# The seam between two stages of a one-core decoder layer: rotary rows, first loads, last stores and four merge tiles change their places

## The chip, the core and the metric

The kernel runs on one core of a Trainium2 chip. A core has a matrix engine (TensorE, PE in the profile), a vector engine (VectorE, DVE), a scalar engine (ScalarE, ACT), a general one (GpSimd, POOL) and a sync engine (SyncE, SP) that here does nothing but issue transfers. Each engine works through its own list of instructions in order; semaphores hold it up where it needs another's result. ACT and POOL can issue transfers too. The metric is the device time of one execution in microseconds; the number that counts is the median of several runs.

## What is computed

One layer of a decoder. x has 1024 rows of 1024 channels; 16 learned rows are put ahead of them, so L = 1040.

```python
h = rms_norm(h_res, pre_norm_g)
z = h @ w_in                       # 1024 x 7328, cut into branches and gates
y_a = (pool_mixer(pv, ...) * silu(pg)) @ w_out_pool
y_b = (mla_attention(cq, ckv, kr, ...) * silu(mg)) @ w_out_mla
y_c = (conformer_conv(cu, ...) * silu(cg)) @ w_out_conf
y_d = (short_conv(sbcx, ...) * silu(sg)) @ w_out_sc
m = sum_i sigmoid(gl_i + bias_i) * y_i
out = h_res + rms_norm(m @ w_o, post_norm_g)     # the 16 rows are dropped
```

The attention has 8 heads of 64 + 32 channels, the 32 being rotary: a rotated key part that all heads share. It is causal, and its softmax is exact (the row maximum is taken off).

## The kernel before, in words

All matmuls are done in a split form: an operand is written as a rounded part and a rest, and three matmuls make one product. The work has three stages, each recorded first and then put in order by a planner.

*Stage one* makes z: 28 pairs of column blocks, each by a scheme of seven block products instead of eight (`unit`, line 578). The last 16 pairs are the merge gates: 32 tiles `th` of 128 channels by 1024 rows, a tanh by ACT each, stored to DRAM by `out_gate` (line 682). Its line 689 issues those stores from ACT, but for the last pair (g == 30) from POOL. Beside the products run the convolutions, the pooling, the queries, keys and values, and the splitting of later weights. Branch results (`bo`), `q`, `k`, the shared rotary key rows `kr`, and `v` with its ones all go through DRAM.

*Stage two* (from line 1244) is the attention, 8 heads by two halves of 512 queries: `seq` (line 1451). For each, `maxima` (line 1302) takes row maxima of the scores: PE, then DVE with a mask made by POOL, then a transpose on PE and a copy by ACT into four further rows of the query tile `qt`. Then `attend` (line 1339): scores, exp, the split of the probabilities, the product with the values. `load_q` fetches a query tile (three buffers), `load_kv` (line 1290) a head's keys `kt` (two buffers), rotary rows and values `vt` (two buffers). The rotary rows are loaded once for each key buffer: for h == 0 into the first, for h == 1 into the second, there with the two halves of the rows exchanged. Between the steps of the attention runs the merge of the three other branches, the generator `fills` (line 1417): 48 steps, each six matmuls (`ps_y`) and an evacuation by DVE with the gate tile `th`. A gate tile and a weight tile `whl` serve two steps; `load_bo` fetches the branch's two operands of 1024 KB each. `refill` (line 1455) hands out the steps evenly over the attention and, with `plan.ahead(-400)`, behind the attention in priority.

*Stage three* merges the attention's branch and makes the output product.

**The planner** (`Plan`, line 194). `record` notes each operation with its engine, a cost, its dependencies and a priority, the number of the record less what `ahead` adds. `behind` (line 248) makes everything recorded inside it wait for the last PE operation recorded so far; lines 1483 to 1490 use it so that the loads for the next head and the next but one query tile don't run ahead of the attention's current step. `flush` (line 334) goes through time, gives each engine the ready operation of the lowest number that `fits`, and emits all operations in that order; stage one is emitted whole before stage two. `fits` (line 367) keeps back a transfer of SP or ACT while the eighth last such transfer has not landed by the planner's reckoning (`landed`, line 417); transfers of POOL are left out of that list. The reason lies in the program: each transfer that SP or ACT issues takes one of eight completion semaphores in turn, and waits until the one that had it before has landed; POOL's take others.

Memory is laid out by pools, and stage two's tiles lie where stage one's lay. A load into such a place waits until the last work there is over.

Of the kernel before, what the change touches and what calls it, by code (L numbers as in the profile page):

```python
# [14 lines left out]

# [49 lines left out]
def f(ap):  # L65
    return ap.bitcast(F32)
# [127 lines left out]
class Plan:  # L194
# [139 lines left out]
    def flush(self):  # L334
# [26 lines left out]
        def slot(b, t):  # L361

            free = [sl for sl in b.group["slots"] if not sl["live"] and sl["after"] <= t]
            if free and (b.group["any"] or b.group["order"][b.group["next"]] is b):
                return min(free, key=lambda sl: (sl["after"], sl["i"]))

        def fits(o, t):

            if o["op"] == "dma_start" and o["eng"] != "POOL" and len(self.landed) >= 8 and self.landed[-8] > t:
                return False  # L370
            return all(slot(b, t) for b in o["bufs"] if not b.live and b.group)

        while events:
            t = events[0][0]
            while events and events[0][0] <= t:
                _, kind, i = heapq.heappop(events)
                if kind == 0:
                    o = self.ops[i]
                    bisect.insort(ready[o["eng"]], (o["prio"], o["i"]))
                elif kind == 2:  # L380
                    for b in self.ops[i]["bufs"]:
                        b.left -= 1
                        if b.left == 0 and b.group:
                            b.slot["live"], b.slot["after"] = None, t
            for e in self.free:
                if self.free[e] > t:
                    continue
                o = next((self.ops[i] for _, i in ready[e] if fits(self.ops[i], t)), None)
                if o is None:
                    if e == "PE" and self.idle and self.ops[self.idle[1]]["end"] is None:  # L390
                        order.append(self.idle[0])
                        self.free[e] = t + 160
                        heapq.heappush(events, (self.free[e], 1, 0))
                    continue
                ready[e].remove((o["prio"], o["i"]))
                for b in o["bufs"]:
                    if not b.live:
                        b.live = True
                        if b.group:
                            b.slot = slot(b, t)  # L400
                            b.slot["live"] = b
                            b.group["next"] += 1
                o["start"] = t
                if o["turns"]:
                    o["cost"] += max(0, self.port[{"DVE": "POOL", "POOL": "DVE"}[e]] - t) * 0.7
                    self.port[e] = t + o["cost"]
                self.free[e] = t + o["cost"]
                o["end"] = t + o["cost"] + self.WAKE[e]
                if o["op"] == "dma_start":
                    if self.pipe is None:  # L410
                        self.pipe = max((x["done"] for x in self.ops if x["op"] == "dma_start"
                                         and "done" in x and x["start"] <= t), default=0)
                    o["done"] = self.pipe = max(self.pipe, t) + o["bytes"]
                    land = self.pipe + o["bytes"] + 4500 + min(0, o["extra"])
                    o["end"] = land + max(0, o["extra"])
                    if o["eng"] != "POOL":
                        self.landed.append(land)
                    heapq.heappush(events, (land, 1, 0))
                for b in o["bufs"]:
                    b.last = max(b.last, o["end"])  # L420
                order.append(o)
                heapq.heappush(events, (self.free[e], 1, 0))
                heapq.heappush(events, (o["end"], 2, o["i"]))
                for u in o["users"]:
                    u["need"] -= 1
                    same = u["eng"] == e and o["op"] != "dma_start"
                    u["at"] = max(u["at"], self.free[e] if same else o["end"])
                    if not u["need"]:
                        heapq.heappush(events, (u["at"], 0, u["i"]))
# [8 lines left out]
def trunk_kernel(ctx, tc, a):  # L438
    nc = tc.nc
    plan = Plan(nc)  # L440
    PE, ACT, DVE, POOL, SP = (plan.engine(e) for e in ("PE", "ACT", "DVE", "POOL", "SP"))
# [7 lines left out]
    def ld(out, in_):  # L449
        SP.dma_start(f(out) if out.dtype == F32R else out, f(in_) if in_.dtype == F32R else in_)  # L450
# [38 lines left out]
    th_dram = [dram.tile([P, NT], F32, name=f"th{i}") for i in range(32)]  # L489
# [6 lines left out]
    kr_dram = dram.tile([32, 2, L], F32R, name="kr")  # L496
# [136 lines left out]
    def full(to, x, ps):  # L633

        if x is None:
            copy(to, ps)
        else:
            add(DVE, to, ps, x)

    def pairs_of_halves(n, each, store):  # L640

        z = {}

        def out(i, j, ps, x, tmp):
            first = i not in z
            if first:
                z[i] = up.tile([P, 2, n], F32, tag="z", bufs=2, name="z")
            m = ps.shape[0]
            each(i, z[i][:m, j], ps, x, tmp)
            if not first:  # L650
                store(i, z[i][:m])
        return out
# [11 lines left out]
    def row(t):  # L664
        return t.rearrange("p j n -> p (j n)")
# [16 lines left out]
    def out_gate(g):  # L682

        def each(i, to, ps, x, tmp):
            if x is not None:
                full(to, x, ps)
            ACT.activation(to, ps if x is None else to, AF.Tanh, scale=0.5,
                           bias=par[:, R_GB + g + i:R_GB + g + i + 1])
        return pairs_of_halves(512, each, lambda i, t: (POOL if g == 30 else ACT).dma_start(th_dram[g + i], row(t)))

# [587 lines left out]
    def load_q(h, c):  # L1280
        qt[h, c] = qk.tile([NA, 2, 512], F32R, tag="q", bufs=3, name="qt")
        ld(qt[h, c][:QK].rearrange("p s n -> p (s n)"), q_dram[c][h].rearrange("p s n -> p (s n)"))

    load_q(0, 0)
    kt = [qk.tile([NA, 2, L], F32R, name=f"kt{i}") for i in range(2)]
# [4 lines left out]
    def load_kv(h):  # L1290
        e, k_, v_ = h % 2, kt[h % 2], vt[h % 2]
        ld(k_[:64].rearrange("p s n -> p (s n)"), k_dram[h // 2][64 * e:64 * (e + 1)].rearrange("p s n -> p (s n)"))
        if h == 0:
            ld(k_[64:96], kr_dram)
        if h == 1:
            ld(k_[64:80], kr_dram[16:])
            ld(k_[80:96], kr_dram[:16])
        v = v_dram[h // 4][h % 4]
        ld(v_[:, 0:8].rearrange("p j c -> p (j c)"), v[:, 0:8].rearrange("p j c -> p (j c)"))
        ld(v_[:NM, 8], v[:NM, 8])  # L1300
# [95 lines left out]
    op, smg = {}, {}  # L1396
# [53 lines left out]
    fill = fills()  # L1450
    seq = [(h, c) for h in range(H) for c in range(2)]
    NUNIT = 16 * 7
    count = {"u": 0, "f": 0}

    def refill():
        count["u"] += 1
        while count["f"] < min(48, 48 * count["u"] / (NUNIT - 2)):

            with plan.ahead(-400):
                next(fill, None)  # L1460
            count["f"] += 1
# [9 lines left out]
    def lead_to(i, n=0):  # L1471

        while lead["i"] <= min(i, len(seq) - 1) or lead["steps"] < n:
            if next(steps, "end") == "end":
                lead["steps"] = math.inf
            lead["steps"] += 1

    load_kv(0)
    load_q(*seq[1])
    lead_to(0)  # L1480
    units = 0
    for i, (h, c) in enumerate(seq):
        with plan.behind():
            if i + 2 < len(seq):
                load_q(*seq[i + 2])
            if c == 0 and h + 1 < H:
                load_kv(h + 1)
            if c == 0 and h % 2:
                smg[h] = at.tile([P, NT], F32, tag="smg", name="smg")
                ld(smg[h], z_dram[f"mg{h // 2}"])  # L1490
        for _ in attend(h, c):
            units += 1
            lead_to(-1, min(5 + units * 10 / 14, 5 * (i + 3)))
            refill()
        lead_to(i + 1)
        with plan.ahead(-300):
            if h == H - 1:
                head_out(h, c, sums_pe(h, c))
            elif c:
                for k, rb in enumerate(sums(h)):  # L1500
                    head_out(h, k, rb)
# [82 lines left out]
    for d in (0, 4, 1, 5, 2, 6, 3, 7):  # L1584
# [3 lines left out]
        for c in range(2):  # L1588
            t = th[:, 512 * c:512 * (c + 1)]
# [23 lines left out]
    def half(name, bufs=4):  # L1613
        return ep.tile([P, 512], F32, tag=name, bufs=bufs, name=name)
# [71 lines left out]
    for t in range(4):  # L1686

        parts = [slice(0, 512)] if t < 3 else [slice(0, 256), slice(256, 512)]
        g = half("g", 1) if t == 3 else a_[t]
# [45 lines left out]
```

## Time and profile before

| | us |
|---|---|
| median of 3 runs | 1018.12 |
| lowest, highest | 1017.72, 1019.06 |
| the profiled execution | 1017.58 |
| its span, first to last instruction | 1015.9 |
| PE busy | 990.5 |
| PE's last matmul of stage one ends | 651.6 |
| PE works on stage three alone from | 883.4 |

The execution is 1.7 us longer than its span. The line numbers of the profile are of no use here: the planner issues every operation from line 332, so the groups are told apart by tiles. A row of the timeline holds the start, the length, the engine, the operation with output and inputs, the count, and in brackets how long the engine stood before it and what it waited for. `SPq`, `ACTq` mark the issue of a transfer, and the length there is that of the issue alone. A row of waits holds who waited for whom, the total in us, how often, and the longest.

### The profile page before, as it was taken

To read this page: it belongs to the slowest core of one execution; us is meant where nothing else is said; L and a number is where in the kernel's file an instruction comes from. 1 tells how busy PE (TensorE), PEld (TensorE's weight loads), DVE (VectorE), ACT (ScalarE), POOL (GpSimd) and SP (SyncE) were. 2 spreads that over 40 slices of the span, in tenths; PEclk is the share of its full clock that TensorE was granted. 3 is DMA by queue.
4 is the path that set the end of the run, shared out by engine and by line. 5 is a ranking of instruction groups with operands and counts; after the bars stand their busy time and mean duration, and the time that the engine had idled before them with its cause. 6 is when DMAs were issued, how large, how long until landed. Compare 5 with 4: busy or idle time off the path is not lost.

```text
span 1015.9 us, 15303 instructions
## 1 busy us (share of the span) xinstructions
PE 990.5 (98%) x5139; PEld 831.7 (82%) x5139; DVE 668.1 (66%) x1106; ACT 455.4 (45%) x911; POOL 685.6 (67%) x640
## 2 busy tenths in 40 slices
PE   9999999999999999999999999989999999799996
PEld 9999898889888878887877888868887878588885
DVE  6754795997999499435455453255565675598747
ACT  7632234443354544444534444136556556224632
POOL 6767867766777666768776765125678876556956
PEclk9999999999999999999999999989999999899998
DMA  7278755679767856566656456877568671662634
GB/s 246 75 229 277 245 169 182 217 226 301 250 214 224 288 189 206 188 197 203 206 175 197 136 172 191 310 206 241 147 188 256 183 209 53 201 228 89 202 120 165
DMA packets 126302, 203.13 MB, mean 200 GB/s; under 512 B 19650, under 2 KB 79161, under 8 KB 124880
## 3 DMA queue, kind: packets, MB, share of 16 engines
q1 hardware_dynamic: 121600, 185.38, 58.2%
q10 hardware_dynamic: 4336, 15.73, 4.2%
q8 instruction: 40, 0.66, 0.3%
q0 software_dynamic: 288, 1.05, 0.3%
q14 instruction: 38, 0.31, 0.1%
HBM read 128.40 MB, written 73.72 MB: 199 GB/s over the span
## 4 chain that ended last, share of the span: by engine, by line
PE 91%; DVE 4%; issue 2%; DMA 1%; POOL 1%; ACT 1%; SPq 0%; DVEq 0%; POOLq 0%; ACTq 0%
PE ps_pa L332 16%; PE ps_pb L332 16%; PE ps_pc L332 15%; PE ps_o L332 10%; PE ps_y L332 8%; PE ps_s L332 7%; PE ps_pd L332 7%; PE ps_u L332 7%; PE ps_x L332 4%; DMA kt<-kr 1%; DVE x L332 1%; DVE a L332 1%; DMA x<-in_x_dram 0%; DVE ps_w L332 0%; DVE ss L332 0%
## 5 line engine op out<-in xcount | busy, mean ns | idle before, releaser
L332 PE MATMUL ps_pb<-T,S 128*128 128x512 f32 (+2 forms) x792 | 172.4, 362 | 0.8 <-DVE u L332 0.8
L332 PE MATMUL ps_pa<-B,A 128*128 128x512 f32 (+2 forms) x792 | 172.2, 362 | 0.0
L332 POOL TENSOR_TENSOR S<-ss,S 128x512 fp32r<-128x512 f32 x84 | 110.5, 1328 | 76.9 <-ACT S L332 76.7
L332 PEld LDWEIGHTS ps_pa<-B,A 128*128 128x128 f32 x792 | 134.6, 188 | 24.4 <-issue 0.5
L332 PEld LDWEIGHTS ps_pb<-T,S 128*128 128x128 f32 x792 | 133.8, 188 | 24.4 <-DVE u L332 1.2
L332 POOL TENSOR_TENSOR A<-raw,A 128x512 fp32r<-128x512 f32 x84 | 116.9, 1397 | 48.2 <-ACT A L332 44.7
L332 POOL TENSOR_TENSOR pt<-p,pt 128x512 fp32r<-128x512 f32 (+4 forms) x112 | 103.8, 955 | 43.5 <-PE ps_s L332 20.5
L332 ACT ACTIVATE S<-ss 128x512 fp32r<-128x512 f32 x84 | 50.8, 628 | 115.4 <-DVE ss L332 72.7
L332 PE MATMUL ps_y<-bo,whl 128*128 128x512 f32 x288 | 90.9, 418 | 6.2 <-DVE op L332 4.9
L332 DVE SCALAR_TENSOR_TENSOR ps_w<-conv,par,ps_w 128x512 f32<-128x512 f32 x116 | 87.2, 752 | 2.4
L332 PE MATMUL ps_pc<-B,S 128*128 128x512 f32 (+2 forms) x396 | 87.5, 364 | 0.5 <-DVE z L332 0.5
L332 PE MATMUL ps_pc<-T,S 128*128 128x512 f32 (+2 forms) x396 | 86.4, 363 | 0.4 <-DVE z L332 0.4
L332 PE MATMUL ps_pd<-T,A 128*128 128x512 f32 (+2 forms) x396 | 84.9, 361 | 0.0
L332 PEld LDWEIGHTS ps_pc<-T,S 128*128 128x128 f32 x396 | 67.1, 188 | 13.2 <-issue 1.0
L332 PEld LDWEIGHTS ps_pc<-B,S 128*128 128x128 f32 x396 | 66.8, 188 | 13.2 <-issue 1.0
L332 PE MATMUL ps_o<-pt,vt 128*128 128x512 f32 (+4 forms) x336 | 77.3, 336 | 0.1
L332 PEld LDWEIGHTS ps_pd<-T,A 128*128 128x128 f32 x396 | 66.9, 188 | 11.9
L332 PE MATMUL ps_s<-qt,kt 100*128 100x512 f32 (+4 forms) x336 | 69.4, 326 | 1.0 <-ACT qt L332 1.0
L332 ACT ACTIVATE A<-raw 128x512 fp32r<-128x512 f32 x84 | 52.7, 627 | 37.4 <-PE ps_pd L332 22.9
L332 ACT ACTIVATE p<-ps_s 128x512 f32<-128x512 f32 (+4 forms) x112 | 49.6, 443 | 38.3 <-DVE ps_s L332 15.6
L332 PEld LDWEIGHTS ps_y<-bo,whl 128*128 128x128 f32 x288 | 53.0, 197 | 14.7 <-DVE op L332 5.3
L332 PEld LDWEIGHTS ps_s<-qt,kt 100*128 100x128 f32 (+1 forms) x336 | 54.7, 176 | 12.5 <-ACT qt L332 1.1
(346 smaller groups left out, 1901.8 us busy)
## 6 DMA issues: line engine op xcount, KB each, us to landing
raw<-in_w_in_dram SPq DMA_DIRECT2D x56, 512.0 KB
th<-th SPq DMA_DIRECT2D x32, 512.0 KB
th<-z ACTq DMA_DIRECT2D x30, 512.0 KB
v<-vhl SPq DMA_DIRECT2D x16, 384.0 KB
qt<-q SPq DMA_DIRECT2D x16, 384.0 KB
vt<-v SPq DMA_DIRECT2D x8, 768.0 KB
bo<-bo SPq DMA_DIRECT2D x6, 1024.0 KB
kt<-k SPq DMA_DIRECT2D x8, 520.0 KB
```

Source lines behind the costliest of these rows:

```text
L332: getattr(self.handle[o["eng"]], o["op"])(*map(real, o["args"]), **{k: real(v) for k, v in o["kw"].items()})
```

## The change

Five edits. The count of transfers in flight holds start and end of each and counts those that overlap the present moment. All gate stores are issued by ACT. The second key buffer's rotary rows are loaded with the first head's keys. Four merge steps are recorded ahead of the first maxima, at their natural priority. And for the first pass of the attention loop the loads don't wait for PE.

```diff
         def fits(o, t):

-            if o["op"] == "dma_start" and o["eng"] != "POOL" and len(self.landed) >= 8 and self.landed[-8] > t:
+            if o["op"] == "dma_start" and o["eng"] != "POOL" and sum(s <= t < e for s, e in self.landed[-40:]) >= 8:
                 return False
...
                     if o["eng"] != "POOL":
-                        self.landed.append(land)
+                        self.landed.append((t, land))
...
-        return pairs_of_halves(512, each, lambda i, t: (POOL if g == 30 else ACT).dma_start(th_dram[g + i], row(t)))
+        return pairs_of_halves(512, each, lambda i, t: ACT.dma_start(th_dram[g + i], row(t)))
...
         if h == 0:
             ld(k_[64:96], kr_dram)
-        if h == 1:
-            ld(k_[64:80], kr_dram[16:])
-            ld(k_[80:96], kr_dram[:16])
+            ld(kt[1][64:80], kr_dram[16:])
+            ld(kt[1][80:96], kr_dram[:16])
...
-    def refill():
+    def refill(early=False):
+        if early:
+            next(fill)
+            count["f"] += 1
+            return
         count["u"] += 1
...
     load_kv(0)
     load_q(*seq[1])
+    for _ in range(4):
+        refill(True)
     lead_to(0)
     units = 0
     for i, (h, c) in enumerate(seq):
-        with plan.behind():
+        with plan.behind() if i else nullcontext():
             if i + 2 < len(seq):
                 load_q(*seq[i + 2])
             if c == 0 and h + 1 < H:
```

More of the change, by code (lines that the diff above doesn't have):

```diff
@@ L13 @@
 import re
-from contextlib import ExitStack, contextmanager
+from contextlib import ExitStack, contextmanager, nullcontext
 import concourse.bass as bass
```

## Prediction, made before the changed kernel was run

> **What bounds the kernel now.** I read the page, then the windows by stage, then the waits of PE, then the timeline around the place that the diff edits.
>
> ```profile
> span 1015.9 us, 15303 instructions
> PE 990.5 (98%) x5139; PEld 831.7 (82%) x5139; DVE 668.1 (66%) x1106; ACT 455.4 (45%) x911; POOL 685.6 (67%) x640
> 100.00:651.60 551.60, 549.27 (x2670) 456.75 (x2669) 362.74 (x499) 234.44 (x443) 381.71 (x342) 1.00 0.67 212
> 640.00:651.60 11.60, 11.60 (x53) 9.41 (x52) 2.07 (x3) 2.14 (x3) 0.77 (x1) 1.00 0.97 359
> 651.60:690.00 38.40, 35.30 (x162) 28.14 (x162) 19.24 (x57) 13.45 (x28) 14.11 (x24) 0.91 0.66 198
> 674.00:681.40 7.40, 7.40 (x29) 6.01 (x29) 2.09 (x8) 1.18 (x2) 0.00 (x0) 0.54 0.43 131
> PE ps_s L332 <- DMA kt<-kr: 2.2, 1, 2.2
> ```
>
> The columns of a window are its length, then busy time and count of PE, PEld, DVE, ACT and POOL, then granted clock, DMA share, GB/s. TensorE bounds the kernel: 990.5 of 1015.9 us. Only time in which PE stands still, or runs at a lower clock, can be won. Stage one ends for PE at 651.6 and is full: 2.3 us idle in the 551.6 us before. The seam behind it, 651.6 to 690, loses 38.4 - 35.3 = 3.1 us idle, 2.2 of them in one wait for the rotary rows of the second key buffer, and then runs 7.4 us at a clock of 0.54, which is 0.46 x 7.4 = 3.4 us more. So the seam costs 6.5 us. That is all that the edits there can give, and PE must have data at 651.6 for it.
>
> **What the load queue does at the seam.** SP's and ACT's DMA issues around the end of stage one (start, length, engine, issue), and what SP waited for at four of them:
>
> ```profile
> 606.46 0.38 SPq L332 DMA_DIRECT2D raw<-in_w_in_dram  x1
> 611.41 0.33 ACTq L332 DMA_DIRECT2D th<-z  x1
> 612.50 0.32 SPq L332 DMA_DIRECT2D bo<-bohi  x1
> 612.99 0.38 SPq L332 DMA_DIRECT2D raw<-in_w_in_dram  x1
> 614.19 0.34 ACTq L332 DMA_DIRECT2D th<-z  x1
> 613.88 0.32 SPq L332 DMA_DIRECT2D bo<-cgt  x1
> 630.87 0.33 ACTq L332 DMA_DIRECT2D th<-z  x1
> 633.65 0.33 ACTq L332 DMA_DIRECT2D th<-z  x1
> ...
> 614.25 0.42 SPq L332 DMA_DIRECT2D qt<-q  x1
> 614.72 0.51 SPq L332 DMA_DIRECT2D kt<-k  x1
> 615.71 0.98 SPq L332 DMA_DIRECT2D kt<-kr  x1
> 618.62 0.30 SPq L332 DMA_DIRECT2D qt<-q  x1
> 631.48 1.02 SPq L332 DMA_DIRECT2D whl<-w_out_pool  x2
> 634.25 4.22 SPq L332 DMA_DIRECT2D vt<-v  x2
> 638.57 0.37 SPq L332 DMA_DIRECT2D bo<-bo  x1
> ...
> SPq L332 <- DMA bo<-bohi: 0.5, 1, 0.5
> SPq L332 <- DMA raw<-in_w_in_dram: 1.9, 1, 1.9
> SPq L332 <- DMA th<-z: 1.3, 1, 1.3
> SPq L332 <- DMA th<-z: 3.6, 1, 3.6
> L332 SPq DMA_DIRECT2D vt<-v x2: 318/318/319, 634.3 to 638.2; - x2
> ```
>
> The first block holds stage one's last eight DMAs of SP and ACT, the second the first loads of stage two, numbered 1 qt, 2 kt, 3 kr, 4 qt, 5 and 6 whl, 7 and 8 vt, 9 bo. None of the four waits is about data: the third load waits for the third of the eight above it (bo), the fourth for the fourth (raw), the seventh and eighth (vt) for the seventh and eighth (the stores of th). Four times of four, a load waits until the DMA eight places before it has landed. ACT's stores count, and they count at their place in the program: stage one is emitted whole before stage two, so a store that runs late stands ahead of loads that could run early. The two stores issued by POOL do not count: they came later than bo, and bo went at 638.57 without them. Line 369 says the same, the eighth last DMA that isn't POOL's must have landed.
>
> **Part by part.**
>
> ```profile
> 650.61 0.77 POOL L332 DMA_DIRECT2D th<-z  x1 [16.38 <-ACT z L332]
> 649.57 0.73 ACT L332 ACTIVATE z<-z,par 128x512 f32<-128x512 f32 x1 [2.81 <-DVE z L332]
> 652.35 0.72 ACT L332 ACTIVATE z<-z,par 128x512 f32<-128x512 f32 x1 [2.05 <-DVE z L332]
> DMA to landing us min/median/max: 3.0/3.4/3.9
> 652.89 10.25 PE L332 MATMUL ps_y<-bo,whl 128*128 128x512 f32 x44
> 657.67 0.17 POOL L332 MEMSET mx<- 128x12 f32 x2
> 661.03 0.31 DVE L332 CUSTOM_DVE_ANT_0 ps_s<-ps_s,maskS 128x144 f32<-128x144 f32 x1
> 666.03 1.89 PE L332 MATMUL ps_s<-qt,kt 100*128 100x512 f32 x9 [0.42 <-ACT qt L332]
> 866.00:884.00 18.00, 11.80 (x51) 8.93 (x50) 11.81 (x12) 3.12 (x9) 7.28 (x8) 0.81 0.81 274
> vt<-v SPq DMA_DIRECT2D x8, 768.0 KB
> bo<-bo SPq DMA_DIRECT2D x6, 1024.0 KB
> th<-th SPq DMA_DIRECT2D x32, 512.0 KB
> whl<-w_out_pool SPq DMA_DIRECT2D x8, 256.0 KB
> ```
>
> *Rotary rows early, first loads not behind PE.* Adds no instruction. Two loads of rotary rows move into the first load of keys, and the loads of the next query, keys and values no longer wait for the first maxima. I take their buffers, but for the values', to be as free as those of loads 1 to 4; then they go in between: 5 and 6 become the rotary rows, 7 and 8 likely qt and kt of the next head. The 2.2 us wait goes, and with it the reason for the low clock. Worth up to 6.5 us if nothing else comes late.
>
> *Four merge tiles ahead of the maxima.* The same 24 matmuls of 10.25/44 = 0.233 us, 5.6 us, and four evacuations, now first. Before, 48 of them ran here anyway, since POOL's mx was ready only at 657.8. They need bo and whl to be there at 651.6.
>
> *Stores by ACT.* POOL loses a queue of 16.38 us in which it waited for ACT's tanh, so its masks are ready before 651.6. ACT gains two issues of 0.33 us, in a stretch where it stood 2.81 and 2.05 us before its last two tanh. The DMA page of the Trainium skill (DMA: Bandwidth & Descriptors, Issuing engines are not separate DMA queues) says that DMAs of all engines end on the same 16 DMA engines and that the issuer matters only for issue time. By that rule this edit is worth nothing; the four waits above speak against it, for the issuer decides whose place in the count of eight is taken.
>
> *Count of eight by times.* The planner no longer sees stores that start later than t as in flight, so in its plan loads 7 and on go early. The waits in the program don't follow it. In stage one it can shift the order a little; PE's idle time there, 2.3 us, bounds a gain, and I take nothing either way, with 2 us as the cost if a weight load slips. In stage two the order of everything can shift; the other hole, 866 to 884 with 6.2 us idle and a clock of 0.81, can shrink or grow by a few us and stays out of the sum.
>
> **The sum.** With the two last stores in the count, they stand directly ahead of stage two, so its seventh load waits for the first and its eighth or ninth for the second. ACT's tanh end at 649.57 + 0.73 = 650.3 and 652.35 + 0.72 = 653.1. A store lands 3.4 us after issue (POOL's) to 4.5 (ACT's at 633.65, which let vt go at 638.2): 653.7 and 656.5, or 1.1 later. SP issues in order, so whl, vt and bo, which went from 631.48 to 638.57, and th behind them wait. From 656.5 two whl, one vt and two bo are 512 + 768 + 2048 = 3328 KB, 3.4 MB; at the 359 GB/s of 640 to 651.6 that is 9.5 us: the second bo lands at 666.0. Bounds: if whl and vt slip through after the first store, only bo is left, 5.8 us, 662.3; if the second vt stands ahead too, 2.2 more, 668.2. I take 666.0.
>
> PE then stands from 651.6 to 666.0, less the three matmuls on the first bo (0.7): 13.7 us (10.0 to 15.9). The restart at the low clock: 3.4, as in the row of 674. The chain of the first maxima, 661.03 to 666.03 or 5.0 us, now has only the fifth and sixth merge tile (2.8 us) and the next maxima as cover: 1.0 (0 to 2.2). What the seam lost before goes: -6.5. Sum 13.7 + 3.4 + 1.0 - 6.5 = **+11.6 us** (6.9 to 15.0). Against the profiled execution's 1017.58 that is 1029.2; the median of the runs is 0.54 above that execution, so 1029.7 (1025.0 to 1033.1).
>
> On the restart, the skill's page TensorE: Matmul & The Clock Gate (What's actually happening) says that the clock halves after an idle window of about 3.4 us and returns after a busy one as long. The trace differs: a wait of 2.2 us was enough, and the low stretch took 7.4 us. By the page the restart would cost 1.7 instead of 3.4 and the sum be +9.9.
>
> **The rivals.**
> *The seam closes (faster).* If the loads of the first merge tiles stand ahead of the stores in the count, or no wait comes of it, PE works on from 651.6, masks are ready, the rotary rows too. Gain 6.5 less the 1.0 of the chain: 1012.6 (1011.6 to 1016). For it: every other edit takes away a wait that the trace shows. Against: bo was the ninth load, and the change puts more ahead of it. It decides by whether bo is issued before 645.
> *A short stall.* Only the first store is in the way: bo goes at 653.7 and lands at 659.5, PE stands 7.2 us, 7.2 + 3.4 - 6.5 = +4.1: 1022 (1018 to 1025).
> *A second stall.* The th tiles come behind bo, 2 x 512 KB or 2.9 us; with two y banks PE halts again and cools again (3.4): +17.9, 1036.
> *No effect.* The planner arrives at nearly the old order: 1018.
>
> **How the numbers follow.** Forecast 0.60, seam closes 0.15, short stall 0.12, second stall 0.08, no effect 0.05. About 0.2% (2 us) is what a measurement of this kernel can tell from no change. Faster 0.15; same 0.05 and 0.03 of the short stall, 0.08; slower 0.77. The predicted time is the forecast's, 1029.7; its own range is 1025.0 to 1033.1. The range 1017.5 to 1036.5 takes in the short stall, no effect and half of the second stall: 0.81.
>
> **What would show it.** Right: SP waits for th<-z some 35 us at the seventh load, bo is issued after 655, PE's first ps_y waits for DMA bo for over 8 us from 651.6, the clock is near 0.5 after it, and the wait for kt<-kr is gone. Wrong: bo issued near 638, ps_y running at 651.6, and the windows from 651.6 to 690 with PE full at clock 1.00. Then the count of eight is not what held vt.

## The result, and the profile after

The changed kernel takes 1034.2 us (median of four runs, 1032.0 to 1034.7) against 1017.9 us for the kernel before (four runs, 1015.4 to 1019.1). The ratio is 1.0159 with an interval of 1.0135 to 1.0183: slower by 16 us. The profiled execution took 1034.46 us. From its page:

```profile
span 1032.7 us, 15314 instructions
PE 993.8 (96%) x5139; PEld 833.4 (81%) x5139; DVE 659.9 (64%) x1106; ACT 455.1 (44%) x911; POOL 686.3 (66%) x638
```

PE does the same 5139 matmuls in 3.3 us more, and the span grows by 16.8. So 13.5 us of it are idle time of PE. The windows of the changed kernel say where (length, then busy time and count of PE, PEld, DVE, ACT and POOL, granted clock, DMA share, GB/s):

```profile
651.60:690.00 38.40, 19.90 (x82) 15.64 (x83) 11.73 (x34) 4.80 (x12) 3.02 (x4) 0.69 0.74 256
651.60:667.40 15.80, 0.00 (x0) 0.00 (x0) 0.00 (x0) 0.45 (x1) 0.00 (x0) 0.55 0.91 308
667.40:677.40 10.00, 7.86 (x18) 5.72 (x19) 1.38 (x2) 0.00 (x0) 0.00 (x0) 0.52 0.78 309
677.40:690.00 12.60, 12.05 (x65) 9.93 (x64) 10.36 (x32) 4.35 (x11) 3.02 (x4) 1.00 0.49 149
...
770.00:810.00 40.00, 37.12 (x184) 29.57 (x183) 20.25 (x56) 21.61 (x48) 33.53 (x35) 0.91 0.65 201
866.00:884.00 18.00, 17.79 (x92) 14.35 (x91) 13.51 (x30) 8.80 (x20) 10.80 (x11) 1.00 0.35 103
```

For 15.8 us behind stage one PE does not run one matmul, and nor do DVE and POOL, while the DMA engines are 91% busy. Then PE runs for 10 us at a clock of 0.52. The seam loses 38.4 - 19.9 = 18.5 us idle and 0.48 x 7.86 = 3.8 by the clock, 22.3 us, against 6.5 before: 15.8 of the 16.8 us. The other two rows are of stretches behind the seam, where the changed kernel is some 16 us late, so that the same time does not hold the same work. The hole of 866 to 884 is gone (6.2 us idle and some 0.19 x 11.80 = 2.2 by the clock before; PE's longest wait behind 800 us is now 1.7 us, at 896.5), and a new one has opened at 770 to 810 (2.9 idle and some 0.09 x 37.12 = 3.3 by the clock, where before 0.9 was idle at a clock of 1.00).

What the engines waited for, in the changed kernel (SP's row is that of 620 to 656, PE's are those of the whole span):

```profile
SPq L332 <- DMA th<-z: 33.3, 4, 13.1
...
PE ps_y L332 <- DMA bo<-bo: 19.0, 2, 16.8
PE ps_s L332 <- DVE mx L332: 2.7, 3, 1.5
PE ps_s L332 <- ACT qt L332: 1.7, 4, 0.6
```

The wait for the rotary rows (`kt<-kr`) is gone from PE's list, and in its place stands one for `bo`, almost nine times as long. The timeline of the changed kernel, SP's and ACT's issues and PE, tells how it came about:

```profile
618.87 0.33 SPq L332 DMA_DIRECT2D qt<-q  x1
619.29 0.50 SPq L332 DMA_DIRECT2D kt<-k  x1
619.85 0.57 SPq L332 DMA_DIRECT2D kt<-kr  x1
620.51 12.26 SPq L332 DMA_DIRECT2D qt<-q  x2
638.53 13.70 SPq L332 DMA_DIRECT2D kt<-kr  x2
652.28 0.48 SPq L332 DMA_DIRECT2D kt<-k  x1
655.79 0.82 SPq L332 DMA_DIRECT2D whl<-w_out_pool  x2
656.71 1.79 SPq L332 DMA_DIRECT2D vt<-v  x4
658.59 1.00 SPq L332 DMA_DIRECT2D bo<-bo  x1
659.64 0.66 SPq L332 DMA_DIRECT2D th<-th  x1
660.40 0.45 SPq L332 DMA_DIRECT2D bo<-bo  x1
...
649.31 0.33 ACTq L332 DMA_DIRECT2D th<-z  x1
652.08 0.33 ACTq L332 DMA_DIRECT2D th<-z  x1
...
647.63 2.94 PE L332 MATMUL ps_pc<-B,S 128*128 128x512 f32 x12
667.40 1.65 PE L332 MATMUL ps_y<-bo,whl 128*128 128x512 f32 x3 [16.84 <-DMA bo<-bo]
671.19 7.75 PE L332 MATMUL ps_y<-bo,whl 128*128 128x512 f32 x21 [2.14 <-DMA bo<-bo]
```

Two issues drawn together in one row are as far apart as the row is long: the second of the two `kt<-kr` goes out where the row ends, just ahead of `kt<-k` at 652.28. It had to wait until the store of 649.31 had landed, and `whl` at 655.79 until the store of 652.08 had. These are the seventh and the ninth load. By the completion semaphores in the trace the first load, `qt`, has its place between the two stores, so here stage one was not emitted quite whole before stage two, and the later store bears on the ninth load and not on the eighth. The first `bo` goes out at 658.59 (638.57 before) and lands at 667.40, the second at 671.19.

### The profile page after: what moved, and what is told of

It reads as the page before. It is cut to its first block, busy times and chain, and to the rows that moved or that the text cites. A ratio compares the mean times of both kernels' runs of the same rounds, so it can differ in the third digit from the quotient of the medians.

```text
span 1032.7 us, 15314 instructions
## 1 busy us (share of the span) xinstructions
PE 993.8 (96%) x5139; PEld 833.4 (81%) x5139; DVE 659.9 (64%) x1106; ACT 455.1 (44%) x911; POOL 686.3 (66%) x638
## 4 chain that ended last, share of the span: by engine, by line
PE 92%; DVE 4%; DMA 2%; issue 1%; ACT 1%; SPq 0%; POOL 0%; DVEq 0%; POOLq 0%; ACTq 0%
PE ps_pb L332 16%; PE ps_pa L332 16%; PE ps_pc L332 15%; PE ps_o L332 10%; PE ps_s L332 8%; PE ps_y L332 8%; PE ps_pd L332 7%; PE ps_u L332 7%; PE ps_x L332 4%; DMA bo<-bo 1%; PE ps_w L332 1%; DVE ps_w L332 1%; DMA whl<-w_out_mla 1%; DVE a L332 1%; SPq L332 0%
## 5 line engine op out<-in xcount | busy, mean ns | idle before, releaser
L332 POOL TENSOR_TENSOR S<-ss,S 128x512 fp32r<-128x512 f32 x84 | 113.1, 1359 | 76.1 <-ACT S L332 70.7
```

Of the source, the lines that this page charges most:

```text
L332: getattr(self.handle[o["eng"]], o["op"])(*map(real, o["args"]), **{k: real(v) for k, v in o["kw"].items()})
```

## The experiments

Theories: **A**, places: ACT's last stores take two of eight places ahead of stage two, and loads that the planner thinks free wait for them. **B**, crowding: the loads of the second head, no longer behind PE, stand ahead of `bo`. **C**, order on PE: the four merge tiles, recorded first, wait for `bo`, where the maxima could have run. **D**, the new count makes a bad order by itself. All times are medians, each ratio against the kernel before on the same chip, with its interval.

### Undoing one part of the change

*The last pair's stores issued by POOL again; the other four parts stay* (e1; edit against the changed kernel):

```diff
-        return pairs_of_halves(512, each, lambda i, t: ACT.dma_start(th_dram[g + i], row(t)))
+        return pairs_of_halves(512, each, lambda i, t: (POOL if g == 30 else ACT).dma_start(th_dram[g + i], row(t)))
```

> The changed kernel with the last pair's stores given back to POOL, all else as changed. Theory A (places: a load waits until the DMA eight places before it has landed, and ACT's two last stores take two of these places): with the stores out of the count the seventh and eighth load wait for the stores of 630 and 633 only, bo is issued by about 641, PE stands under 2 us between 651 and 690, and the time is 1011 to 1014. Theory B (crowding: the second head's keys, values and query, loaded ahead of bo, make bo late): bo is still late by most of its 20 us, 1025 or more. Theory C (PE's order: the merge tiles ahead of the maxima take away what PE could do while bo is late): as B, 1025 or more.

1014.35 us, 0.9984 (0.9963 to 1.0005). The loss is gone with this one line. The issue of `kt<-k` and `bo`, and PE, in this kernel's timeline:

```profile
638.56 0.48 SPq L332 DMA_DIRECT2D kt<-k  x1
642.23 0.37 SPq L332 DMA_DIRECT2D bo<-bo  x1
...
651.75 0.94 PE L332 MATMUL ps_y<-bo,whl 128*128 128x512 f32 x3 [0.79 <-DMA bo<-bo]
655.56 7.64 PE L332 MATMUL ps_y<-bo,whl 128*128 128x512 f32 x21 [2.87 <-DMA bo<-bo]
```

SP still waits 15.8 us here, for the two ACT stores of some 630 and 633 us, and `bo` is 3.7 us late for PE: B costs something here, but it is not the loss.

*The old count; the other four parts stay* (e3):

```diff
-            if o["op"] == "dma_start" and o["eng"] != "POOL" and sum(s <= t < e for s, e in self.landed[-40:]) >= 8:
+            if o["op"] == "dma_start" and o["eng"] != "POOL" and len(self.landed) >= 8 and self.landed[-8][1] > t:
```

> The changed kernel with the old count (the eighth last DMA must have landed), all else as changed, ACT's stores too. Theory A: the stores keep their places, so it stays slow, 1022 to 1034. Theory D: the new count was the cause, so the time goes back to 1012 to 1018.

1021.0 us, 1.0044 (1.0024 to 1.0064): some 5 us slower, not 16, and between what A and D expected. PE never waits for `bo` in the seam; it is 34.07 us busy there at a clock of 0.87. So the other four parts with the old count lose little over a quarter of what the change loses, less than A had it.

*The four merge tiles not ahead of the maxima* (e5):

```diff
-    for _ in range(4):
-        refill(True)
```

> The changed kernel with the merge tiles not recorded ahead of the maxima, all else as changed, ACT's stores and the new count too. Theory A: bo is issued near 658 as before, the stall begins a little later, since PE first does the first maxima (about 1 us of matmuls) and then comes to matmuls that wait for bo or vt: 1027 to 1034. Theory C (PE's order makes the loss): PE goes through the maxima and the first attention steps while bo is late, 1016 to 1022.

1034.47 us, 1.0172 (1.0136 to 1.0207): as slow as the change. PE does its first maxima tile and then stands as long:

```profile
651.53 0.58 PE L332 MATMUL ps_s<-kt,qt 96*128 96x144 f32 x3
668.85 1.65 PE L332 MATMUL ps_y<-bo,whl 128*128 128x512 f32 x3 [16.74 <-DMA bo<-bo]
```

C falls: with this count the planner places merge tiles there anyway.

*Only the very last store issued by POOL* (e7):

```diff
-        return pairs_of_halves(512, each, lambda i, t: ACT.dma_start(th_dram[g + i], row(t)))
+        return pairs_of_halves(512, each, lambda i, t: (POOL if g == 30 and i == 0 else ACT).dma_start(th_dram[g + i], row(t)))
```

> The changed kernel with only the very last store (about 652) given to POOL; the one before it (about 649) stays with ACT. Theory A: the wait for the later store goes, whl is issued at about 652.5 instead of 655.8 and bo at about 655.4 instead of 658.6: 3 us less than the changed kernel, 1029 to 1032. If only the number of DMAs in flight mattered, not the place: either half of the loss goes (1026) or none (1034).

1030.51 us, 1.0133 (1.0097 to 1.0168). `whl` goes out at 652.66 instead of 655.79, but `bo` at 656.95, 1.6 us earlier, and PE's long wait is 15.5 us instead of 16.8. The other store alone holds the queue until 652:

```profile
652.07 0.48 SPq L332 DMA_DIRECT2D kt<-k  x1
652.66 0.99 SPq L332 DMA_DIRECT2D whl<-w_out_pool  x2
656.95 0.37 SPq L332 DMA_DIRECT2D bo<-bo  x1
```

### One part, or two, on the kernel before

*Only the stores by ACT* (e2; edit: `(POOL if g == 30 else ACT)` becomes `ACT`):

> The kernel before with nothing changed but that ACT issues the last pair's stores too. Theory A: slower, the seventh load waits for the store of about 650 until about 653, bo is issued after 655; as the planner's old count sees this, it puts the attention's first steps ahead of the merge tiles, so PE has more to do meanwhile: 1022 to 1030. Theories B, C and D (the new count makes a bad order): none of their causes is in this kernel, 1018 within 2.

1015.73 us, 0.9987 (0.9968 to 1.0006). A's expectation missed. The places are taken as A says, and SP waits for them (36.5 us between 620 and 670), but PE does not. The timeline of this kernel:

```profile
655.56 0.30 SPq L332 DMA_DIRECT2D qt<-q  x1
662.35 0.84 SPq L332 DMA_DIRECT2D bo<-bo  x2
...
655.72 0.33 ACTq L332 DMA_DIRECT2D th<-z  x1
...
654.04 0.58 PE L332 MATMUL ps_s<-kt,qt 96*128 96x144 f32 x3
659.07 3.19 PE L332 MATMUL ps_s<-qt,kt 100*128 100x512 f32 x9 [0.42 <-ACT qt L332]
674.38 0.64 PE L332 MATMUL ps_y<-bo,whl 128*128 128x512 f32 x2
```

`bo` is issued even later than in the changed kernel. But the old count holds those loads back in the plan too, and the order fits that: the planner puts the first head's maxima, scores and values ahead, whose loads went out at 617 to 639, and PE comes to the first merge tile only at 674.

*Only the new count* (e4; lines 369 and 417 as in the change):

> The kernel before with the new count alone. Theory A: POOL's stores still take no place, so 1018 within 3, with the order of the loads at the seam nearly as before. Theory D: a good part of the 16 us, 1024 or more.

1014.06 us, 0.9966 (0.9943 to 0.9989). D falls: by itself the count wins 0.3%. A part of it lies in stage one: from 100 us to PE's last matmul of that stage PE is idle for 1.3 to 1.4 us in all ten kernels with the new count, and for 2.3 to 2.4 in the four with the old one.

*Stores by ACT and the new count, nothing else* (e10):

> The kernel before with two of the five edits, ACT's stores and the new count; rotary rows, first loads and merge tiles as before. Theory A in its full form (the stores take places, and the count by times hides this from the planner, which with the old count put attention ahead of the merge tiles): whl is ahead of the stall, vt waits for the store of 649 and bo for that of 652, bo is issued near 656 and lands some 6 to 7 us later, PE waits 9 to 12 us for it: 0.5 to 1.0% slower than the kernel before. If the early loads or the merge tiles are needed for the loss: within 0.3% of before.

1030.12 us, 1.0126 (1.0088 to 1.0164). Two edits, of which one is worth nothing and the other a small gain, lose 13 us together. In this kernel's timeline:

```profile
652.10 0.79 SPq L332 DMA_DIRECT2D vt<-v  x2
658.25 0.32 SPq L332 DMA_DIRECT2D bo<-bo  x1
...
663.21 1.65 PE L332 MATMUL ps_y<-bo,whl 128*128 128x512 f32 x3 [12.10 <-DMA bo<-bo]
```

It is the changed kernel's picture, without the rotary rows, the early loads of the second head or the merge tiles. By the ratios, the two apart come to -0.13% and -0.34%, the pair to +1.26%, so 1.7% (18 us) lies in their meeting. With the three other parts the ratio is 1.0159; the intervals of the two overlap, so what those add to the loss can't be told.

### What is worth keeping

*The stores of the last two pairs by POOL, the rest as changed* (e6; `g == 30` of e1 becomes `g >= 28`):

> The changed kernel with the stores of the last two pairs given to POOL, so that no store of 629 to 652 takes a place. Theory A: nothing of stage one holds the seventh and eighth load at 638, the early loads are done before bo's memory is free, bo is issued by 638.5, PE stands under 1 us between 651 and 690 at clock 1.00, and the time is 0.4 to 0.7% below the kernel before. Theory B: the second head's loads still crowd bo, the first merge matmuls wait some 3 us as with the last pair alone on POOL, within 0.2% of the kernel before.

1009.27 us, 0.9922 (0.9894 to 0.9951). Windows and timeline of this kernel:

```profile
651.60:690.00 38.40, 37.98 (x198) 31.11 (x197) 21.67 (x65) 16.15 (x36) 16.77 (x28) 1.00 0.60 197
866.00:884.00 18.00, 16.02 (x69) 12.28 (x68) 9.19 (x11) 4.43 (x10) 11.53 (x12) 0.91 0.74 262
```

```profile
636.62 0.32 SPq L332 DMA_DIRECT2D bo<-bo  x1
650.33 2.96 PE L332 MATMUL ps_y<-bo,whl 128*128 128x512 f32 x12
```

With no late store among the places `bo` goes out at 636.62, and the seam is full: 0.4 us idle at a clock of 1.00, 6.1 us better than before. The tail (second row) has 2.0 us idle, where the kernel before has 6.2.

*The last pair's stores by POOL, and the first pass's loads behind PE as before* (e8; e1 and the line below):

```diff
-        with plan.behind() if i else nullcontext():
+        with plan.behind():
```

> The changed kernel with the last pair's stores given back to POOL and the first pass's loads kept behind PE again, as before; rotary rows early, merge tiles first and the new count stay. Theory B for what is left of the loss with the last pair on POOL (3.7 us of waits for bo): with the second head's query, keys and values out of bo's way bo is issued by 639 and PE does not wait for it; the rotary rows are there, so the time is 0.2 to 0.6% below the kernel before. Theory A for it (the stores of 630 and 633 hold the seventh and eighth load until 638): bo still comes after 641 and PE waits 2 to 4 us, within 0.2% of before.

1008.69 us, 0.9916 (0.9888 to 0.9944): the fastest median here, not to be told from e6. Here `bo` goes out at 639.18 with nothing of the second head's `kt` and `vt` ahead of it; from e1 to e8 only B was taken away, and that is worth some 0.7%.

*Both, e6's stores and e8's line* (e9):

> Stores of the last two pairs by POOL, the first pass's loads kept behind PE as before; rotary rows early, merge tiles first, new count. If both cures act on the same 3.7 us of waits for bo, it is no better than either: 0.7 to 0.9% below the kernel before. If they add up: more than 1.0% below.

1009.12 us, 0.9918 (0.9893 to 0.9944). The two don't add up: each alone already gets `bo` there in time.

*e8 without the four merge tiles ahead* (e11):

> The last pair's stores by POOL, first loads behind PE, rotary rows early, new count, but the merge tiles not ahead of the maxima. If the merge tiles' place is worth nothing once the rotary rows are early and bo is in time: 0.7 to 0.9% below the kernel before, as with them. If it is what closes the seam: 0.2 to 0.5% below, with PE idle over 2 us between 651 and 690.

1013.15 us, 0.9962 (0.9945 to 0.9979). Its seam is as busy as e8's (36.92 us, clock 1.00), but PE's old wait of the tail is back, which e8 does not have:

```profile
PE ps_y L332 <- DVE op L332: 4.9, 1, 4.9
```

From 840 to 900 PE is 53.72 us busy here and 57.51 in e8. So the merge tiles ahead pay some 4 us (1009.12 for e9 on the same chip), and not at the seam but in the tail.

*e8 with the old count* (e12; the line of e3):

> The last pair's stores by POOL, first loads behind PE, rotary rows early, merge tiles first, but the old count. If the new count adds nothing where POOL has the last stores: 0.6 to 0.9% below the kernel before. If it is a part of the gain (alone it gave 0.34%): 0.3 to 0.6% below.

1011.49 us, 0.9937 (0.9915 to 0.9959), beside e8's 0.9916 on another chip: the intervals overlap, so what the new count is worth here in time stays open; in stage one PE is idle for 2.4 us here and for 1.3 in e8.

## Why the prediction was right, and where its sizes were off

The slowdown, its place and the wait behind it came as forecast. The time, 1034.2, is 4.5 us above the forecast's 1029.7: past the end of its own range (1033.1), inside the wide one (to 1036.5).

- *TensorE bounds; the seam can give 6.5 us and no more.* The first half held. The second held at the seam (e6 wins 6.1 there), but not for the edits: e6 and e8 win 7.9 and 8.5 us, where the rival "the seam closes" had 5.5. For e8 the reason is shown by e11: the merge tiles ahead also close part of the tail hole, which I had kept out of the sum. For e6 it is likely the same, but no run tests it.
- *A load waits until the DMA eight places before it has landed, ACT's stores count, POOL's don't.* Shown by e7, e1 and e6: of the last four stores ACT issues four in the change, three in e7, two in e1 and none in e6, and the first `bo` goes out at 658.59, 656.95, 642.23 and 636.62. The rule of the Trainium skill that was weighed there (DMA: Bandwidth & Descriptors, Issuing engines are not separate DMA queues) would have e1 as slow as the change; e1 is 1.75% faster by the two ratios.
- *But places alone cost nothing.* I called the new count worth nothing either way and the ACT stores the cause. That the forecast came out in spite of it is partly luck, since the change has both. e2, e4 and e10 show that it takes both: the places make the wait, and by the order of e2 and e10 the count hides it from the planner. The prediction had said that the planner would no longer see those stores; it had not asked what order a planner that sees them makes.
- *Stores land at 653.7 and 656.5.* At 651.9 and 655.8 at the latest, when SP goes on: 2.6 and 3.7 us from issue.
- *SP waits some 35 us at the seventh load.* 33.3 us, but in four pieces, two of them (11.6 and 5.7) for the stores of the pair before. That the last four stores and not two bear on the first loads I had missed.
- *Bytes ahead of `bo`: 3.4 MB at 359 GB/s, landed at 666.0; PE idle 13.7 (10.0 to 15.9).* This is the term that was mis-sized. PE stood 15.8 + 2.1 = 17.9 us from 651.6 on, beyond the upper bound (and 1.0 more before that, since stage one ended for PE at 650.6, 1.0 us earlier than before). The windows of the changed kernel from the issue of `whl` to the landing of the second `bo`:

```profile
655.80:660.00 4.20, 0.00 (x0) 0.00 (x0) 0.00 (x0) 0.00 (x0) 0.00 (x0) 0.50 0.95 257
660.00:667.40 7.40, 0.00 (x0) 0.00 (x0) 0.00 (x0) 0.00 (x0) 0.00 (x0) 0.50 0.98 384
667.40:671.20 3.80, 1.66 (x4) 0.84 (x4) 0.00 (x0) 0.00 (x0) 0.00 (x0) 0.50 1.01 408
```

  By length times rate they moved 5.47 MB in 15.4 us, 355 GB/s. So the rate was right (359 taken). The bytes were not (3.4 MB taken): ahead of the second `bo` stood two heads' `vt` and a `th`, one `vt` and one `th` or 1.3 MB more than I took. The other 0.8 MB would fit the `whl` and `th` issued behind it; the trace does not tell whose bytes they were.
- *Restart 3.4.* 3.8: the clock is at 0.50 from 654 to 676, 0.76 from 676 to 678, then 1.00. Here the clock took 10 us from the first matmul to come back, some 6 from the second start after a halt of 2.1. The Trainium skill (TensorE: Matmul & The Clock Gate, What's actually happening) has it back after a busy window of about 3.4 us, from which the prediction took an estimated 1.7; the same section says that the window runs freely, so by an estimate from it up to two windows, 6.8 us, can pass, and the some 6 us of this trace lie within that.
- *Chain of the first maxima 1.0.* At most the 0.55 us that PE waited for `qt` in 677.4 to 690.
- *-6.5 for what the seam lost before.* As said; the wait for `kt<-kr` is gone.
- *The sum.* 17.9 + 3.8 + 0.55 - 6.5 = 15.8 instead of 11.6. The 4.2 us between them are PE's wait (17.9 for 13.7); the restart and the chain miss by 0.4 each and cancel. The 1.0 us left to the span's 16.8 is the net of all smaller differences ahead of and behind the seam.
- *The rivals.* The seam does not close in the changed kernel. It does in e6 and e8, but the point from which I let it decide, `bo` issued before 645, was too late: in e1 it went at 642.2 and PE still waited 3.7 us. The short stall is out too: e7, with one store in the way, loses 13 us and not 4. The second stall, the `th` tiles, is not there as a halt; `th` counted as bytes.

## What to carry to other kernels

Where completion semaphores are handed out in turn, a transfer that runs late blocks the load that gets the same one, however free that load's own data and buffer are; so keep late stores off the engines that share them, or see that the planner of the order counts them as the program does. A model made more accurate in one respect can be worse where it hides a wait that is real: test such an edit together with those that lean on it, since neither of the two that lost 13 us here lost anything alone. And read a late load by the queue ahead of it, place by place and byte by byte, not by its own transfer time.

## What the runs showed of the hardware that was not expected

The clock fell with much shorter pauses than the one at the seam. Between 789.9 and 794.1 us PE of the changed kernel waited once 0.81 and once 1.54 us, with work in between; the clock fell at 793.0, half a microsecond into the second wait, and in 795 to 800 it was 0.51. Its windows:

```profile
790.00:795.00 5.00, 2.69 (x12) 1.70 (x12) 4.93 (x14) 0.60 (x1) 3.76 (x5) 0.80 0.99 403
795.00:800.00 5.00, 4.55 (x12) 3.38 (x12) 2.38 (x7) 2.98 (x5) 2.48 (x3) 0.51 1.02 275
```

The low stretches have a common measure. In windows of 0.1 us the clock is at 0.50 from 673.9 to 680.8 and from 871.9 to 878.8 in the kernel before, and from 793.0 to 799.9 and, at the seam, from 653.1 to 677.0 in the changed one: three times some 6.83 us, and once 23.89, which is seven halves of 6.83. The two falls lie 198.0 us apart in the one kernel and 139.9 in the other, 58 and 41 times the half of 6.83. So in these two traces the clock changed only on a grid of some 3.41 us; what must happen within one step of it, they don't settle.

And the tail hole of the kernel before begins with one addition on DVE that took 5.82 us, where the same operation takes 0.69 a little later (timeline of the kernel before, below). POOL worked without a pause from 863.0 to 872.2. The Trainium skill's page SBUF — State Buffer (Who interferes with whom) tells of a port that the two share, and of an instruction that waits whole until the other's is over. That would fit; no run here tests it.

```profile
866.91 5.82 DVE L332 TENSOR_TENSOR m<-m,th 128x512 f32<-128x512 f32 x1
...
874.19 0.69 DVE L332 TENSOR_TENSOR m<-m,th 128x512 f32<-128x512 f32 x1
```
